# Broadcasting the reciprocal RMS of a window: from two TensorE transposes and a ScalarE copy to a round trip through DRAM

## The chip, the cores and the metric

The kernel runs on one core of a Trainium2 chip. The metric is the device time of one execution in microseconds (us). TensorE is written PE here, VectorE DVE, ScalarE ACT, GpSimd POOL and SyncE SP, as the profile writes them.

## The reference

One inference step of a two-layer decoder trunk, for a prompt of 4096 tokens and a sample group of 8 sequences with 4 tokens each; the model width is 1024. Both layers begin with an RMS norm over the 1024 features of each token, and it is the factor of this norm that the change sends another way:

```
def rms_norm(x, g):
    xf = x.astype(jnp.float32)
    y = xf * lax.rsqrt(jnp.mean(xf * xf, axis=-1, keepdims=True) + NORM_EPS)
    return (y * g.astype(jnp.float32)).astype(x.dtype)
```

Layer 0 projects the normed input to an S5 branch (a diagonal complex recurrence over the tokens, followed by GELU and a gated unit) and to a GLA branch (gated linear attention in chunks of 64 tokens), joins the two, projects them back and adds the residual. Layer 1 projects to 16 query heads and 2 key and value heads, applies norms and a rotary embedding, attends within a window of 128 tokens with a sink per head, multiplies with a gate, projects back and adds the residual. Weights and activations are float32 at the border; the kernel splits each operand of a projection into a high and a low float16 part and multiplies three of the four products.

## The kernel before, in words

The activations lie with the features on the partitions and the tokens along the free axis. A window is 256 tokens (`NW`), of which the prompt has 16; the 1024 features of one window are four chunks of 128 partitions by 2 by 256 float32, 256 KB each.

The program has three phases. **Phase 0** (up to about 420 us, with loads to about 600) computes the weights' scales, the S5 tables, the S5 projection of all windows (`stage`, then `ustream`) and the S5 scan. `stage` also computes the reciprocal RMS of each window of the input and keeps it in `rst0`, with the tokens on the partitions: column 2w holds the first 128 tokens of window w, column 2w+1 the others. **Phase 1** (about 600 to 1750 us) goes through the windows of layer 0; the end of a window (`outstream`) writes the layer's result to DRAM (`h1_d`), sums its squares, and `stats` and `rms` keep the reciprocal RMS for layer 1 in `rst1`. **Phase 2** (about 1800 us to the end) goes through the windows of layer 1, with input chunks loaded from `h1_d`.

A window begins with `prep`. Four input chunks, which were loaded when the window before began, have to be multiplied by the reciprocal RMS of their tokens. Since tokens lie along the free axis there, the 256 factors are needed as a row on all 128 partitions. `rbcast` (L294 to L304) makes that tile, `rb`: two PE transposes (L300) of a `rst` column, broadcast along its free axis, into a PSUM tile, and one ACT copy (L303) to SBUF. `xsplit` (L306 to L318) then handles each chunk in three steps: DVE multiplies it by `rb` (L313), ACT rounds it to the high part `xh` (L314), POOL subtracts to get the low part `xl` (L315). All projections of the window read `xh` and `xl` on PE.

The reciprocal RMS itself comes out of `rms` (L285 to L292): a sum of squares on PE, a scale and an offset on DVE (`var`, L291), and a power of -1/2 on POOL (`rst`, L292).

Each engine executes its own instructions in order. The order is set when the program is built: `merge` interleaves generators that stand for streams of work by the costs that they yield, and a scheduler then places each instruction on its engine by modelled times. Tiles come from pools with a number of buffers each; an instruction that writes a tile waits until the last reader of the buffer's former content is done. SP issues nearly all the DMAs, and it does so in order as well: a DMA whose source or buffer isn't ready holds up every DMA behind it.

Of the kernel before, what the change touches and what calls it, by code (L numbers as in the profile page):

```python
# [106 lines left out]
class K:  # L107
# [166 lines left out]

    def stats(self, acc, n, rst, blk0, wp, pp, tag="misc"):

        nc = self.nc
        nc.gpsimd.tensor_add(acc[:, 0, 0:n], acc[:, 0, 0:n], acc[:, 1, 0:n])
        m = min(n, 128)
        ps = pp.tile([128, 512], F32, name=tag)  # L280
        for i in range((n + 127) // 128):
            nc.tensor.matmul(ps[0:m, i:i + 1], acc[:, 0, i * 128:i * 128 + m], self.onesf[:, 0:1], start=True, stop=True)
        self.rms(ps, n, rst, blk0, wp)

    def rms(self, ps, n, rst, blk0, wp):  # L285

# [316 lines left out]
    def phase0(self):  # L603
# [50 lines left out]
        for k in range(KT):  # L654
            nc.scalar.activation(wuh[:, k], st[k], AF.Copy, bias=0.0, scale=gs[:, k:k + 1])
            nc.vector.scalar_tensor_tensor(wul[:, k], st[k], gs[:, k:k + 1], wuh[:, k],
                                           op0=OP.mult, op1=OP.subtract)

        def stage(c0, n, blk0, xs=None):

# [3 lines left out]
            for c in range(4):  # L664
# [169 lines left out]
    def phase1(self, es0, tail):  # L834
# [90 lines left out]
        def prep(w):  # L925
            rb = self.rbcast(self.rst0, 2 * w, n, Pb, pmi, tag="pt")
            Ws[w]["x"] = self.xsplit(Ws[w]["x"], n, rb, hp)
            if w + 1 < NWIN:
                Ws[w + 1]["x"] = self.xload(xp, I["xT"], n * (w + 1), n)

        def gate_a(w):
# [424 lines left out]
        def outstream(W, w):  # L1356
# [91 lines left out]
    def phase2(self, es1, tail):  # L1448
# [703 lines left out]
```

## Time and profile before

| what | value |
|---|---|
| median of 3 runs | 3215.05 us (3214.31 to 3219.88) |
| the profiled execution's own time | 3223.62 us |
| its span, first to last instruction | 3221.8 us |
| mean granted TensorE clock | 0.975 |
| PE busy | 3048.6 us, 95% of the span |
| DVE busy | 2016.0 us, 63% |
| ACT busy | 1504.0 us, 47% |
| POOL busy | 1304.7 us, 40% |
| hardware DMA queue, share of 16 engines | 36.5% |

The times of the three runs and that of the profiled execution belong to the same kernel; the profiled one is 8.57 us above the median. Busy shares are means over the whole span, in which phase 0 differs from the other two phases: there PE, DVE and POOL take turns as the busiest engine, while PE is the busiest by far in phases 1 and 2.

### The profile page before, as it was taken

How to read it: one execution, taken by the hardware profiler on the slowest of the kernel's cores; microseconds unless marked ns; L12 is line 12 of the kernel's file. 1: busy time of each engine (PE TensorE's matmuls, PEld its weight loads, DVE VectorE, ACT ScalarE, POOL GpSimd, SP SyncE). 2: the span in 40 equal slices, each digit the busy share in tenths (PEclk: the TensorE clock that was granted, in tenths of full speed). 3: DMA queues.
4: the chain of work that ended last, by engine and by line, in shares of the span. 5: the costliest groups of instructions: out<-in, count | busy, mean ns of one | idle time of the engine just before them, and what ended most of it. 6: DMA issues, size and time to landing. Idle time of an engine off the chain costs nothing. (4 is left out here: it accounts for less than half of the span.)

```text
span 3221.8 us, 65657 instructions
## 1 busy us (share of the span) xinstructions
PE 3048.6 (95%) x25501; PEld 2351.8 (73%) x25501; DVE 2016.0 (63%) x4881; ACT 1504.0 (47%) x3954; POOL 1304.7 (40%) x1324
## 2 busy tenths in 40 slices
PE   6898878899999999999999999999999999999998
PEld 5687766678888777788877666777677777777777
DVE  8869998744444443444446567666666666666666
ACT  4386557343343443333345345444445454444444
POOL 7823232222222211222222555555555555555562
PEclk9699989999999999999999989999999999999999
DMA  4288467622222222322224325333333333333333
GB/s 131 56 233 195 97 143 195 185 54 56 53 54 57 55 52 65 71 57 53 50 49 138 100 48 129 80 79 80 75 75 77 79 74 80 74 81 79 82 77 77
DMA packets 583467, 285.57 MB, mean 89 GB/s; under 512 B 396497, under 2 KB 556193, under 8 KB 583009
## 3 DMA queue, kind: packets, MB, share of 16 engines
q1 hardware_dynamic: 583152, 281.36, 36.5%
q8 instruction: 200, 3.28, 0.4%
q14 instruction: 115, 0.93, 0.1%
HBM read 164.94 MB, written 53.23 MB: 68 GB/s over the span
## 5 line engine op out<-in xcount | busy, mean ns | idle before, releaser
L315 POOL TENSOR_TENSOR xl<-x,xh 128x512 f16<-128x512 f32 (+1 forms) x196 | 261.3, 1356 | 301.3 <-ACT xh L314 273.5
L1687 ACT ACTIVATE Sc<-Sc,ng,rq 128x128 f32<-128x128 f32 x512 | 245.8, 482 | 163.7 <-DVE ng L1681 159.6
L326 PE MATMUL mm<-ogh,woh 128*128 128x256 f16 x960 | 261.5, 273 | 3.5 <-ACT vf L1627 3.0
L327 PE MATMUL mm<-ogl,woh 128*128 128x256 f16 x960 | 261.6, 273 | 0.0
L328 PE MATMUL mm<-ogh,wol 128*128 128x256 f16 x960 | 261.6, 273 | 0.0
L273 POOL TENSOR_TENSOR acc<-acc,sq 128x512 f32<-128x512 f32 x48 | 62.4, 1300 | 489.7 <-ACT sq L272 489.7
L1716 POOL TENSOR_TENSOR Pp<-Sc,Pp 128x512 f16<-128x512 f32 x128 | 151.9, 1188 | 210.3 <-ACT Pp L1715 200.9
L326 PEld LDWEIGHTS <-woh 128*128 128x128 f16 x2112 | 207.4, 98 | 39.8 <-issue 10.4
L327 PEld LDWEIGHTS <-woh 128*128 128x128 f16 x2112 | 207.4, 98 | 38.6 <-issue 9.8
L337 PEld LDWEIGHTS <-xl 128*128 128x128 f16 x1536 | 150.9, 98 | 111.7 <-issue 15.3
L328 PEld LDWEIGHTS <-wol 128*128 128x128 f16 x2112 | 207.2, 98 | 28.0 <-issue 4.8
L335 PEld LDWEIGHTS <-xh 128*128 128x128 f16 x1536 | 151.2, 98 | 99.3 <-issue 13.4
L336 PEld LDWEIGHTS <-xh 128*128 128x128 f16 x1536 | 151.1, 98 | 89.4 <-issue 5.9
L1723 DVE TENSOR_TENSOR PC<-PT,mT 128x1024 f16<-128x1024 f16 x128 | 100.4, 784 | 162.6 <-DMA PT<-Pp 158.3
L314 ACT ACTIVATE xh<-x 128x512 f16<-128x512 f32 (+1 forms) x196 | 118.1, 618 | 118.9 <-DVE x L313 102.9
L326 PE MATMUL mm<-xh,wuh 128*128 128x256 f16 (+1 forms) x544 | 151.1, 282 | 10.3 <-ACT us L728 4.9
L327 PE MATMUL mm<-xl,wuh 128*128 128x256 f16 (+1 forms) x544 | 150.5, 282 | 6.9 <-POOL xl L315 6.9
L313 DVE TENSOR_TENSOR x<-x,rb 128x512 f32<-128x512 f32 (+1 forms) x188 | 138.4, 789 | 20.9 <-ACT rb L303 12.9
L328 PE MATMUL mm<-xh,wul 128*128 128x256 f16 (+1 forms) x544 | 150.5, 282 | 0.0
L1715 ACT ACTIVATE Pp<-Sc 128x512 f16<-128x512 f32 x128 | 80.1, 626 | 141.0 <-issue 115.9
L328 PE MATMUL mm<-xh,wi1gal 128*128 128x256 f16 x512 | 141.1, 276 | 4.0 <-DVE wi1gal L246 4.0
L326 PE MATMUL mm<-xh,wi1qkh 128*128 128x256 f16 x512 | 140.2, 274 | 4.8 <-DVE gb L963 4.8
(724 smaller groups left out, 10487.8 us busy)
## 6 DMA issues: line engine op xcount, KB each, us to landing
x<-in_xT SPq DMA_DIRECT2D x128, 256.0 KB
wst<-in_w_in SPq DMA_DIRECT2D x64, 256.0 KB
xr<-in_xT SPq DMA_DIRECT2D x64, 256.0 KB
h_d<-xr SPq DMA_DIRECT2D x64, 256.0 KB
x<-h_d SPq DMA_DIRECT2D x64, 256.0 KB
xr<-h_d SPq DMA_DIRECT2D x64, 256.0 KB
out_yT<-xr SPq DMA_DIRECT2D x64, 256.0 KB
wst<-in_w_out SPq DMA_DIRECT2D x48, 256.0 KB
```

Of the source, the lines that this page charges most:

```text
L313: nc.vector.tensor_mul(x, x, rb[:, None, :].to_broadcast([128, 2, n]))
L314: nc.scalar.activation(h, x, AF.Copy, bias=0.0, scale=1.0)
L315: nc.gpsimd.tensor_sub(l, x, h)
L326: nc.tensor.matmul(ps, wh[:, k0 + k, c], xh[k], start=(k == 0), stop=False)
L327: nc.tensor.matmul(ps, wh[:, k0 + k, c], xl[k], start=False, stop=False)
L328: nc.tensor.matmul(ps, wl[:, k0 + k, c], xh[k], start=False, stop=(k == n - 1))
L335: nc.tensor.matmul(ps, xh[k][:, t], wh[:, k, c0:c1], start=(k == 0), stop=False)
L336: nc.tensor.matmul(ps, xh[k][:, t], wl[:, k, c0:c1], start=False, stop=False)
L337: nc.tensor.matmul(ps, xl[k][:, t], wh[:, k, c0:c1], start=False, stop=(k == n - 1))
L1687: nc.scalar.activation(Sc[:, i], Sc[:, i], AF.Exp, bias=ng[:, i:i + 1], scale=scale[:, i:i + 1], accum_out=de[:, i:i + 1])
L1716: nc.gpsimd.tensor_sub(Pp[:, 1], Sc, Pp[:, 0])
L1723: nc.vector.tensor_mul(PC, PT, mT[:, None, :].to_broadcast([128, 8, 128]))
```

## The change

`rms` gets a destination. When it has computed the factors of a window other than window 0, POOL issues a DMA that writes the window's two columns to a DRAM row of 256 float32 (`rs0` for layer 0, `rs1` for layer 1). That is 15 writes in phase 0 and 15 in phase 1, of 256 elements of 4 bytes each (the column pair is read with the partition as the inner axis). A new function `rbload` reads such a row to all 128 partitions by a DMA on SP, whose source has a step of 0 along the partitions: 1 KB of DRAM becomes a tile of 128 KB. `prep` of phases 1 and 2 takes this tile in place of the result of `rbcast`. In phase 1 it is loaded a window ahead, right behind the four input chunks; in phase 2 the program loads it in `prep` itself. `rb` has one buffer.

`rbcast` is still used for window 0 of phases 1 and 2, for the `split` of phase 0 (all 16 windows of the S5 projection) and for both sample groups.

```
--- before.py
+++ after.py
@@ -272,7 +272,7 @@
             nc.scalar.activation(sq, x, AF.Square, bias=0.0, scale=1.0)
             nc.gpsimd.tensor_add(acc[:, :, 0:n], acc[:, :, 0:n], sq)
 
-    def stats(self, acc, n, rst, blk0, wp, pp, tag="misc"):
+    def stats(self, acc, n, rst, blk0, wp, pp, tag="misc", dst=None):
 
         nc = self.nc
         nc.gpsimd.tensor_add(acc[:, 0, 0:n], acc[:, 0, 0:n], acc[:, 1, 0:n])
@@ -280,9 +280,9 @@
         ps = pp.tile([128, 512], F32, name=tag)
         for i in range((n + 127) // 128):
             nc.tensor.matmul(ps[0:m, i:i + 1], acc[:, 0, i * 128:i * 128 + m], self.onesf[:, 0:1], start=True, stop=True)
-        self.rms(ps, n, rst, blk0, wp)
-
-    def rms(self, ps, n, rst, blk0, wp):
+        self.rms(ps, n, rst, blk0, wp, dst)
+
+    def rms(self, ps, n, rst, blk0, wp, dst=None):
 
         nc = self.nc
         nb = (n + 127) // 128
@@ -290,6 +290,14 @@
         v = wp.tile([128, 2], F32, name="var")
         nc.vector.tensor_scalar(v[0:m, 0:nb], ps[0:m, 0:nb], 2.0**-20 / D, 2.0**-20 * EPS, op0=OP.mult, op1=OP.add)
         nc.gpsimd.tensor_tensor(rst[0:m, blk0:blk0 + nb], v[0:m, 0:nb], self.mhalf[0:m, 0:nb], op=OP.pow)
+        if dst is not None and nb == 2 and blk0:
+            nc.gpsimd.dma_start(dst[blk0 // 2].rearrange("b p -> p b"), rst[:, blk0:blk0 + 2])
+
+    def rbload(self, d, pool, bufs=1):
+
+        rb = pool.tile([128, NW], F32, name="rb", bufs=bufs)
+        self.nc.sync.dma_start(rb, bass.AP(tensor=d.tensor, offset=d.offset, ap=[[0, 128], [1, NW]]))
+        return rb
 
     def rbcast(self, rst, blk0, n, wp, pp, tag="misc", rtag="rb", **kw):
 
@@ -656,6 +664,9 @@
             nc.vector.scalar_tensor_tensor(wul[:, k], st[k], gs[:, k:k + 1], wuh[:, k],
                                            op0=OP.mult, op1=OP.subtract)
 
+        self.rs0 = [self.dr.tile([2, 128], F32, name=f"rs0_{w}") for w in range(NWIN)]
+        self.rs1 = [self.dr.tile([2, 128], F32, name=f"rs1_{w}") for w in range(NWIN)]
+
         def stage(c0, n, blk0, xs=None):
 
             xs = xs or self.xload(xp, I["xT"], c0, n)
@@ -682,7 +693,7 @@
                     for i in range((n + 127) // 128):
                         nc.tensor.matmul(ps[0:m, i:i + 1], sq[:, a, 128 * i:128 * i + m], self.onesf[:, 0:1],
                                          start=(c + a + i == 1), stop=(c + a == 4), skip_group_check=True)
-            self.rms(ps, n, self.rst0, blk0, wp)
+            self.rms(ps, n, self.rst0, blk0, wp, self.rs0)
 
             def split():
                 rb = self.rbcast(self.rst0, blk0, n, wp, pms)
@@ -923,10 +934,11 @@
         n = NW
 
         def prep(w):
-            rb = self.rbcast(self.rst0, 2 * w, n, Pb, pmi, tag="pt")
+            rb = Ws[w]["rb"]
             Ws[w]["x"] = self.xsplit(Ws[w]["x"], n, rb, hp)
             if w + 1 < NWIN:
                 Ws[w + 1]["x"] = self.xload(xp, I["xT"], n * (w + 1), n)
+                Ws[w + 1]["rb"] = self.rbload(self.rs0[w + 1], Pb)
 
         def gate_a(w):
             W = Ws[w]
@@ -1367,7 +1379,7 @@
                 if c == 0:
                     W["r"].append(self.xchunk(P, I["xT"], 3, n * w, n, name="xr", bufs=3))
             yield 0.1
-            self.stats(acc, n, self.rst1, 2 * w, P, pms, tag="pt")
+            self.stats(acc, n, self.rst1, 2 * w, P, pms, tag="pt", dst=self.rs1)
 
         def glu(w, early):
             W = Ws[w]
@@ -1409,6 +1421,7 @@
         Ws = [{} for _ in range(NWIN)]
         Ws[0]["x"] = x0
         Ws[1]["x"] = self.xload(xp, I["xT"], n, n)
+        Ws[1]["rb"] = self.rbload(self.rs0[1], Pb)
         merge((instream(0), 42.0), (loads(), 20.0))
 
         def some(g, n):
@@ -1528,7 +1541,7 @@
         self.vf = None
 
         def prep(w):
-            rb = self.rbcast(self.rst1, 2 * w, n, Pa, ptt, tag="pt")
+            rb = self.rbload(self.rs1[w], Pa)
             Ws[w]["x"] = self.xsplit(Ws[w]["x"], n, rb, hp)
             if w + 1 < NWIN:
                 Ws[w + 1]["x"] = self.xload(xp, self.h1_d, n * (w + 1), n)

```

(The prompt's window 0 keeps the old way since `x0` of phase 0 is passed on, and the first window of phase 2 is handled apart.)

Counted over the built programs, the change takes away 60 PE transposes (24183 matmuls become 24123) and 30 ACT copies, and adds 30 DMAs on SP (1197 become 1227) and 30 DMAs on POOL, which issued none before. Lines behind the new code move: L313 is L321 in the changed kernel, L315 is L323, L1354 is L1366.

The scheduler places the remaining instructions anew. Three places follow; numbers behind a name tell buffers and values apart.

The first is DVE at the end of a window of phase 1, where the residual chunks `xr` of this window are summed and the input chunks `x` of the next are multiplied by `rb`. Before:

```order
L1354 SCALAR_TENSOR_TENSOR xr_11522<-mm_12177,sob_5387,xr_11522 128x512
L1354 SCALAR_TENSOR_TENSOR xr_11524<-mm_12243,soa_5411,xr_11524 128x512
L1354 SCALAR_TENSOR_TENSOR xr_11524<-mm_12281,sob_5387,xr_11524 128x512
L1354 SCALAR_TENSOR_TENSOR xr_12080<-mm_12341,soa_5411,xr_12080 128x512
L313 TENSOR_TENSOR x_11472<-x_11472,rb_12372 128x512
L313 TENSOR_TENSOR x_11474<-x_11474,rb_12372 128x512
L313 TENSOR_TENSOR x_11476<-x_11476,rb_12372 128x512
L313 TENSOR_TENSOR x_11478<-x_11478,rb_12372 128x512
L1354 SCALAR_TENSOR_TENSOR xr_12080<-mm_12405,sob_5387,xr_12080 128x512
L1103 COPY_PREDICATED attm0_5376<-mk_5372,pa0_12687 128x256
```

In the changed kernel:

```order
L1366 SCALAR_TENSOR_TENSOR xr_10630<-mm_11356,soa_5458,xr_10630 128x512
L1366 SCALAR_TENSOR_TENSOR xr_10630<-mm_11394,sob_5434,xr_10630 128x512
L321 TENSOR_TENSOR x_11504<-x_11504,rb_11510 128x512
L321 TENSOR_TENSOR x_11506<-x_11506,rb_11510 128x512
L1366 SCALAR_TENSOR_TENSOR xr_11193<-mm_11454,soa_5458,xr_11193 128x512
L321 TENSOR_TENSOR x_11508<-x_11508,rb_11510 128x512
L1366 SCALAR_TENSOR_TENSOR xr_11193<-mm_11515,sob_5434,xr_11193 128x512
L321 TENSOR_TENSOR x_12422<-x_12422,rb_12430 128x512
L1068 SCALAR_TENSOR_TENSOR A_11604<-A_11604,z_11559 128x256
```

The block of four multiplications is taken apart: they stand between the `xr` rows, each behind its own chunk's load, and the first chunk of the window after next (`x_12422`, with the next `rb`, `rb_12430`) follows at once. On SP, `rb_12430` stands behind the load of `x_12422`, and behind it the store of `xr_11193` to `h1_d`, a load of `xr` and four loads of `z`; as `rb` has one buffer, that DMA waits for the multiplication of `x_11508`.

The second is DVE in a window of phase 2, where the softmax of a block (`mx`, `ng`, `sn`, `de`, `Sc`) stands among the multiplications. Before:

```order
L313 TENSOR_TENSOR x_24068<-x_24068,rb_25249 128x512
L313 TENSOR_TENSOR x_24070<-x_24070,rb_25249 128x512
L313 TENSOR_TENSOR x_24072<-x_24072,rb_25249 128x512
L1712 COPY_PREDICATED Sc_25279<-mkc_20886,pt_25280 128x256
L1767 SCALAR_TENSOR_TENSOR og_25093<-po_25080,ga_23923 128x256
L1767 SCALAR_TENSOR_TENSOR og_25093<-po_25080,ga_23984 128x256
L1712 COPY_PREDICATED Sc_25279<-mkc_20886,pt_25291 128x256
L1712 COPY_PREDICATED Sc_25473<-mkc_20886,pt_25474 128x256
L1677 TENSOR_REDUCE mx_25302<-Sc_25279 128x4
L1712 COPY_PREDICATED Sc_25473<-mkc_20886,pt_25485 128x256
L1678 TENSOR_TENSOR mx_25302<-mx_25302,rq_24146 128x4
L313 TENSOR_TENSOR x_24074<-x_24074,rb_25249 128x512
```

In the changed kernel:

```order
L1690 TENSOR_REDUCE mx_27707<-Sc_27684 128x4
L321 TENSOR_TENSOR x_26482<-x_26482,rb_27654 128x512
L1691 TENSOR_TENSOR mx_27707<-mx_27707,rq_26554 128x4
L1692 TENSOR_TENSOR mx_27707<-mx_27707,snk_20901 128x4
L1780 SCALAR_TENSOR_TENSOR og_27501<-po_27488,ga_26334 128x256
L1780 SCALAR_TENSOR_TENSOR og_27501<-po_27488,ga_26395 128x256
L1694 TENSOR_SCALAR ng_27711<-mx_27707 128x4
L1696 TENSOR_TENSOR sn_27713<-ng_27711,snk_20901 128x4
L321 TENSOR_TENSOR x_27676<-x_27676,rb_28923 128x512
L321 TENSOR_TENSOR x_27678<-x_27678,rb_28923 128x512
L1703 TENSOR_TENSOR de_27768<-de_27768,sn_27713 128x4
```

The window's last chunk (`x_26482`, with `rb_27654`) and the first chunks of the next window (`x_27676`, with `rb_28923`) now stand six rows apart, all of one softmax chain. The load of `rb_28923` waits on SP for the multiplication of `x_26482`, the last that reads the one buffer.

The third is POOL in phase 0, where the S5 tables are made (`tv`, `tc`, `tg`) and the low parts of the S5 projection's input. Before:

```order
L315 TENSOR_TENSOR xl_1437<-x_1293,xh_1436 128x512
L292 TENSOR_TENSOR rst0_76<-var_1525,mhalf_74 128x2
L499 TENSOR_TENSOR tv_1148<-Q2_493,R81_665 128x512
L528 TENSOR_TENSOR tc2_529<-CT1_93,sn_445 128x8x32
L492 TENSOR_TENSOR tg_994<-bc_293,Li_119 128x576
L526 TENSOR_TENSOR tc1_528<-ST1_94,sn_445 128x8x32
L499 TENSOR_TENSOR tv_1197<-Q2_493,R81_665 128x512
L492 TENSOR_TENSOR tg_1019<-bc_293,Li_119 128x576
```

In the changed kernel:

```order
L292 TENSOR_TENSOR rst0_76<-var_1560,mhalf_74 128x2
L507 TENSOR_TENSOR tv_1182<-Q2_526,R81_698 128x512
L536 TENSOR_TENSOR tc2_562<-CT1_93,sn_478 128x8x32
L500 TENSOR_TENSOR tg_1028<-bc_325,Li_119 128x576
L534 TENSOR_TENSOR tc1_561<-ST1_94,sn_478 128x8x32
L507 TENSOR_TENSOR tv_1231<-Q2_526,R81_698 128x512
L294 DMA rs0_4_246<-rst0_76 128x2x1
L500 TENSOR_TENSOR tg_1053<-bc_325,Li_119 128x576
L534 TENSOR_TENSOR tc1_561<-ST1_94,sn_478 128x512
```

The write of `rs0_4` stands between two table instructions, six rows behind the power that makes its source; the table instructions themselves stand in nearly the same order.

## Rows read from the trace of the kernel before

**Rows 1.** Busy time of each engine by stretch; its first line names the columns.
```profile
core 0: us, PE busy (x) PEld busy (x) DVE busy (x) ACT busy (x) POOL busy (x), PEclk, DMA share, GB/s
40.00:160.00 120.00, 95.53 (x630) 77.58 (x628) 108.10 (x178) 41.12 (x73) 107.20 (x70) 0.75 0.28 62
160.00:220.00 60.00, 55.36 (x463) 49.58 (x461) 27.77 (x43) 45.16 (x97) 18.82 (x16) 0.91 0.83 220
220.00:420.00 200.00, 169.38 (x1409) 151.23 (x1406) 198.27 (x380) 124.71 (x261) 64.58 (x46) 0.96 0.66 156
600.00:1700.00 1100.00, 1088.82 (x9185) 858.63 (x9182) 483.46 (x1257) 436.26 (x1034) 249.12 (x217) 1.00 0.24 60
1850.00:3222.00 1372.00, 1329.70 (x11411) 976.86 (x11409) 909.48 (x2312) 656.41 (x2064) 732.35 (x836) 0.99 0.37 79
```

**Rows 2.** PE's waits from 600 to 1700 us: waiting line, releaser, us in total, times, longest.
```profile
PE mm L326 <- DVE xr L1354: 4.2, 2, 2.1
PE pt L282 <- POOL acc L278: 3.0, 1, 3.0
...
PE mm L327 <- POOL xl L315: 0.8, 2, 0.5
```

**Rows 3.** PE's waits from 1850 us to the end, the same columns.
```profile
PE po L1761 <- DMA PT<-Pp: 26.8, 22, 3.2
PE mm L326 <- ACT vf L1627: 3.0, 1, 3.0
...
PE mm L337 <- POOL xl L315: 0.8, 1, 0.8
```

**Rows 4.** Timeline of PE, phase 1: start us, us, instruction, count, idle before.
```profile
1004.48 0.27 PE L327 MATMUL mm<-ol,woh 128*128 128x256 f16 x1
1004.59 0.27 PE L328 MATMUL mm<-oh,wol 128*128 128x256 f16 x1
1004.70 0.38 PE L300 MATMUL pt<-identf,rst 128*128 128x128 f32 x2
1004.92 0.27 PE L326 MATMUL mm<-ob,woh 128*128 128x256 f16 x1
1005.03 0.27 PE L327 MATMUL mm<-ob,woh 128*128 128x256 f16 x1
```

**Rows 5.** Timeline of ACT, phase 1.
```profile
1005.12 0.38 ACT L303 ACTIVATE rb<-pt 128x256 f32<-128x256 f32 x1 [2.15 <-PE pt L300]
```

**Rows 6.** Timeline of DVE, phase 1, end of a window.
```profile
997.10 0.75 DVE L1354 SCALAR_TENSOR_TENSOR xr<-mm,sob,xr 128x512 f32<-128x512 f32 x1 [4.24 <-PE mm L328]
1004.90 0.75 DVE L1354 SCALAR_TENSOR_TENSOR xr<-mm,soa,xr 128x512 f32<-128x512 f32 x1 [7.05 <-PE mm L328]
1005.57 3.45 DVE L313 TENSOR_TENSOR x<-x,rb 128x512 f32<-128x512 f32 x4
1008.94 0.74 DVE L1354 SCALAR_TENSOR_TENSOR xr<-mm,sob,xr 128x512 f32<-128x512 f32 x1
```

**Rows 7.** Timeline of SP in phase 2.
```profile
2647.51 6.15 SPq L259 DMA_DIRECT2D x<-h_d  x4
2658.18 1.23 SPq L1718 DMA_TRANSPOSE PT<-Pp  x1
2659.99 0.38 SPq L1807 DMA_DIRECT2D out_yT<-xr  x1
```

**Rows 8.** Timeline of DVE, phase 2, around a chunk's multiplication.
```profile
2646.71 0.75 DVE L1767 SCALAR_TENSOR_TENSOR og<-po,ga 128x256 f32<-128x256 f32 x2
...
2649.02 0.71 DVE L1678 TENSOR_TENSOR mx<-mx,rq 128x4 f32<-128x4 f32 x1
2650.38 0.99 DVE L313 TENSOR_TENSOR x<-x,rb 128x512 f32<-128x512 f32 x1 [0.65 <-DMA x<-h_d]
...
2651.90 0.15 DVE L1679 TENSOR_TENSOR mx<-mx,snk 128x4 f32<-128x4 f32 x1
...
2652.09 0.16 DVE L1681 TENSOR_SCALAR ng<-mx 128x4 f32<-128x4 f32 x1
...
2653.21 0.15 DVE L1683 TENSOR_TENSOR sn<-ng,snk 128x4 f32<-128x4 f32 x1
```

**Rows 9.** Timeline of POOL, phase 0.
```profile
124.48 5.54 POOL L528 TENSOR_TENSOR tc<-CT,sn 128x512 f32<-128x512 f32 x1
...
137.97 0.69 POOL L292 TENSOR_TENSOR rst<-var,mhalf 128x2 f32<-128x2 f32 x1
...
143.38 1.49 POOL L528 TENSOR_TENSOR tc<-CT,sn 128x512 f32<-128x512 f32 x1
```

**Rows 10.** Timeline of SP, phase 0.
```profile
173.03 1.29 SPq L737 DMA_DIRECT2D ud<-us  x2
...
179.51 0.97 SPq L760 DMA_DIRECT2D U<-ud  x2
```

**Rows 11.** Timeline of DVE, phase 0: the last table instruction.
```profile
157.76 0.69 DVE L530 TENSOR_TENSOR ST<-ST,tc 128x512 f32<-128x512 f32 x1
```

**Rows 12.** Page, part 5: the group of the softmax products on DVE.
```profile
L1723 DVE TENSOR_TENSOR PC<-PT,mT 128x1024 f16<-128x1024 f16 x128 | 100.4, 784 | 162.6 <-DMA PT<-Pp 158.3
```

More of the change, by code (lines that the diff above doesn't have):

```diff
@@ L273, in square, with stats @@
             nc.gpsimd.tensor_add(acc[:, :, 0:n], acc[:, :, 0:n], sq)
-    def stats(self, acc, n, rst, blk0, wp, pp, tag="misc"):
+    def stats(self, acc, n, rst, blk0, wp, pp, tag="misc", dst=None):
         nc = self.nc
@@ L282, in stats, with rms @@
             nc.tensor.matmul(ps[0:m, i:i + 1], acc[:, 0, i * 128:i * 128 + m], self.onesf[:, 0:1], start=True, stop=True)
-        self.rms(ps, n, rst, blk0, wp)
-    def rms(self, ps, n, rst, blk0, wp):
+        self.rms(ps, n, rst, blk0, wp, dst)
+    def rms(self, ps, n, rst, blk0, wp, dst=None):
         nc = self.nc
@@ L292, in rms, with rbload @@
         nc.gpsimd.tensor_tensor(rst[0:m, blk0:blk0 + nb], v[0:m, 0:nb], self.mhalf[0:m, 0:nb], op=OP.pow)
+        if dst is not None and nb == 2 and blk0:
+            nc.gpsimd.dma_start(dst[blk0 // 2].rearrange("b p -> p b"), rst[:, blk0:blk0 + 2])
+    def rbload(self, d, pool, bufs=1):
+        rb = pool.tile([128, NW], F32, name="rb", bufs=bufs)
+        self.nc.sync.dma_start(rb, bass.AP(tensor=d.tensor, offset=d.offset, ap=[[0, 128], [1, NW]]))
+        return rb
     def rbcast(self, rst, blk0, n, wp, pp, tag="misc", rtag="rb", **kw):
@@ L657, in phase0 @@
                                            op0=OP.mult, op1=OP.subtract)
+        self.rs0 = [self.dr.tile([2, 128], F32, name=f"rs0_{w}") for w in range(NWIN)]
+        self.rs1 = [self.dr.tile([2, 128], F32, name=f"rs1_{w}") for w in range(NWIN)]
         def stage(c0, n, blk0, xs=None):
@@ L684, in stage @@
                                          start=(c + a + i == 1), stop=(c + a == 4), skip_group_check=True)
-            self.rms(ps, n, self.rst0, blk0, wp)
+            self.rms(ps, n, self.rst0, blk0, wp, self.rs0)
             def split():
@@ L925, in prep @@
         def prep(w):
-            rb = self.rbcast(self.rst0, 2 * w, n, Pb, pmi, tag="pt")
+            rb = Ws[w]["rb"]
             Ws[w]["x"] = self.xsplit(Ws[w]["x"], n, rb, hp)
@@ L929, in prep @@
                 Ws[w + 1]["x"] = self.xload(xp, I["xT"], n * (w + 1), n)
+                Ws[w + 1]["rb"] = self.rbload(self.rs0[w + 1], Pb)
         def gate_a(w):
@@ L1369, in outstream @@
             yield 0.1
-            self.stats(acc, n, self.rst1, 2 * w, P, pms, tag="pt")
+            self.stats(acc, n, self.rst1, 2 * w, P, pms, tag="pt", dst=self.rs1)
         def glu(w, early):
@@ L1411, in phase1 @@
         Ws[1]["x"] = self.xload(xp, I["xT"], n, n)
+        Ws[1]["rb"] = self.rbload(self.rs0[1], Pb)
         merge((instream(0), 42.0), (loads(), 20.0))
@@ L1530, in prep @@
         def prep(w):
-            rb = self.rbcast(self.rst1, 2 * w, n, Pa, ptt, tag="pt")
+            rb = self.rbload(self.rs1[w], Pa)
             Ws[w]["x"] = self.xsplit(Ws[w]["x"], n, rb, hp)
```

## The prediction

> **What bounds the kernel now.** I read the busy time by stretch first [rows 1]. From 600 to 1700 us PE is busy for 1088.82 of 1100 us, from 1850 us to the end for 1329.70 of 1372; the granted clock is 1.00 and 0.99 there, the upper of its two levels. DVE has 483.46 and 909.48 us of work in the same stretches, ACT 436.26 and 656.41, POOL 249.12 and 732.35. So PE sets the time in both phases, and an edit counts there by what it does to PE's stream or to PE's waits. Then I read those waits. In phase 1 they are few, the largest 4.2 us for sums of the residual (`xr`) in two waits [rows 2]; none is for `rb`. In phase 2 one stands out: PE's product `po` waits for the transposed softmax `PT` for 26.8 us, in 22 waits of at most 3.2 us [rows 3]. The group of DVE's products on the same `PT` has 128 members [rows 12], so about one block in six is late. The chain that makes these blocks runs over DVE, ACT, POOL and SP, so what delays DVE in phase 2 can show on PE.
>
> Phase 0 is different. Between 40 and 160 us POOL is busy for 107.20 of 120 us and DVE for 108.10, PE for 95.53 [rows 1]; from 220 to 420 us DVE is busy for 198.27 of 200. Between the two, the 60 us up to 220 have DVE at 27.77 and POOL at 18.82, while the DMAs take a share of 0.83. The tables end on DVE at 158.4 us [rows 11], but S5's first loads of `U` are issued only at 179.5, behind a store of `ud` at 173.0 [rows 10]. The tables are thus ready some 20 us before they are wanted, and the low parts (`xl`) of the S5 projection and the DMAs decide.
>
> **What goes.** On PE, a pair of transposes starts at 1004.70 and the next matmul at 1004.92: 0.22 us of its stream, in which two matmuls of the usual kind would fit [rows 4]. No wait of PE is put down to them in phases 1 and 2. With 60 transposes gone, 30 pairs x 0.22 = 6.6 us leave the bounding engine, 3.3 us per phase. On ACT 30 copies go, 0.38 us each [rows 5], together 11.4 us; ACT has 1100 - 436.26 us free in phase 1 alone, so this is worth nothing by itself. It did wait 2.15 us in order for the transpose, and this wait goes too; but the four multiplications that follow on DVE take 3.45 us [rows 6], and PE waited only 0.8 us for any `xl` in each of the two phases [rows 2, 3]. A shorter way to `xl` therefore gives at most 1.6 us; I take 0.
>
> **What comes: the writes, on POOL.** Thirty DMAs are issued by POOL, which issued none before, so the trace has no price. From below: SP's plain DMA takes 0.38 us to issue [rows 7], if POOL does as well. From above: POOL's instructions sometimes take several times their length, as the 5.54 us for a `tc` that takes 1.49 a few rows on [rows 9]; if a write is stretched by that difference as well, it is 0.38 + 4.05 = 4.4 us. I take the transposing DMA on SP, 1.23 us [rows 7], as the nearest row, since it also scatters single elements. In the stretch in which POOL is nearly full stand four writes (`rs0_2` to `rs0_5`): 1.5, 4.9 or 17.7 us. The 20 us between tables and `U` hide the middle value, as far as it delays tables; the low parts in the same stretch have no such slack that a row shows, so I take 0 and keep 0 to 17.7 us for the range. The other 11 writes of phase 0 and the 15 of phase 1 stand where POOL has most of its time free (249.12 of 1100 us busy), and their results are wanted a phase later. They cost nothing there. Each moves 1 KB.
>
> The Trainium skill speaks against exactly this issue: "SBUF — State Buffer", in "SBUF: two separate sides", says that a DMA issued from POOL has its descriptors made by POOL's cores, which can't write them while DVE runs an instruction that takes both ports; its figures are some 620 ns alone and some 3100 ns beside a DVE copy. The stretched POOL rows in a time of a busy DVE agree in kind [rows 9], though no run here shows a DMA of POOL. By its two figures, called an estimate here, four writes would take 2.5 to 12.4 us, inside the bounds above.
>
> **What comes: the loads, on SP and DVE.** Thirty loads x 0.38 us are 11.4 us of SP's issue time in some 2500 us, and 128 KB each are 3.8 MB where the DMA share is 0.24 and 0.37 [rows 1]. Nothing for these. What counts is the wait: `rb` has one buffer, so its load starts when the last multiplication with the former tile is done, and DVE then stands in order until it has landed. For the time of a load the nearest row is that of the input chunk, 256 KB: the first of a group of four is issued at 2647.51, and the multiplication that waited for one began at 2650.38 [rows 7, 8], so issue and load took at most 2.87 us. I take 2.9 us from the former multiplication's end to the next one's start; the lower bound is half of it, as the transfer has half the bytes.
>
> In phase 1, between the two multiplications (`x_11508` and `x_12422`) stands one sum of `xr`, which waits for PE. In the trace of before such a sum waited 4.24 and 7.05 us for PE [rows 6], more than 2.9. The load lies in the shadow of a wait that is there anyway: 0. Behind it on SP, the store of `xr`, one load of `xr` and four of `z` come later by up to 2.9 us; the `xr` load is the one that PE could come to feel, through a sum of the next window; PE's 4.2 us in two waits for such sums [rows 2] show how seldom they are late, and I take 0.
>
> In phase 2, six rows stand between: two of `mx`, two of `og`, one `ng`, one `sn`. By their rows that is 0.71 + 0.15 + 0.75 (for both `og`) + 0.16 + 0.15 = 1.92 us [rows 8]. DVE would stand 2.9 - 1.9 = 1.0 us in the middle of a softmax chain, with `de` and `Sc` queued behind, on which POOL, the transposing DMA and at last PE's `po` wait. From below it is 0 (the load at half the time). Before, DVE stood 0.65 us there for an input chunk [rows 8], so not all of this is new. With 15 windows that is 15 us for DVE, of which PE feels what falls on a block that is late already: 22 of 128 [rows 3, 12], so 15 x 0.17 = 2.6 us. That is the term I take; the bounds are 0 and 15 us.
>
> **The reordering.** The scheduler shifts matmuls by a few places in all phases. No row prices this. PE's waits of 12 us in phase 1 and some 40 in phase 2 (1100 - 1088.82 and 1372 - 1329.70) are the size of what it can give or take; I take 0 and allow 6 us either way.
>
> **The sum.** -6.6 + 0 + 2.6 = -4.0 us. The profiled execution would go from 3223.62 to 3219.6 us (its span of 3221.8 has 1.8 us around it, which do not change). The median of the runs is 8.57 us below that execution, and I lower it by the same 4.0: 3215.05 - 4.0 = 3211.0 us. That is 0.12%. A measurement of this kernel tells about 0.2% from no change, which is 6.4 us: faster means below 3208.6, slower above 3221.5.
>
> **The rivals.**
> *A larger gain.* The transposes' and the copy's waits in order are gone, multiplications start as soon as a chunk lands, and the softmax chain of the next window finds ACT and DVE free. If a third of PE's 26.8 us for `PT` goes too, it is -6.6 - 8.9 = -15.5: 3199.5 us. For it: DVE's block of 3.45 us is taken apart, and it held up the next sum [rows 6]. Against it: PT's wait has no `rb` in it.
> *The wait for rb decides phase 2.* DVE stands for 1.0 us in each of 15 windows, and each of these delays goes through the softmax chain to PE, in place of one in six: 15 - 6.6 = +8.4: 3223.5 us. It decides from the point where more than 6.6 us of the 15 reach PE, and shows as slower from 13. For it: one buffer, and the chain is the one wait that PE has [rows 3]. Against it: only 22 of 128 blocks are late now.
> *The writes lengthen phase 0.* Four stretched writes at 4.4 us, all on the path through the low parts to `U`: 17.7 - 4.0 = +13.7: 3228.8 us. It shows as slower from 10.4 us on, 2.6 us a write. For it: POOL's 107.20 of 120 us [rows 1]. Against it: the 20 us between the tables and `U` [rows 10, 11].
> *The change doesn't do what it says.* What PE saves it waits for elsewhere, as the chain over DVE, POOL and SP keeps its length: 3215 us. Phase 1 speaks against it, where PE is at 99% [rows 1].
>
> **How the numbers follow.** The forecast has 0.45, the larger gain 0.20, the wait in phase 2 0.15, the writes 0.12, nothing 0.08. Of the forecast's 0.45, with its 6 us either way, 0.18 falls below 3208.6 and 0.26 within the 0.2%, 0.01 above. Faster: 0.18 + 0.20 = 0.38. Same: 0.26 + 0.08 = 0.34. Slower: 0.15 + 0.12 + 0.01 = 0.28. The range runs from 3196 (a little beyond the larger gain) to 3230 us (a little beyond the writes). The forecast's own range is 3205 to 3217.
>
> **What would show it.** Right: PE's busy time in phases 1 and 2 lower by some 6 us; no PE wait on `rb` or its multiplication; the multiplications of phase 1 late by nothing on the `rb` DMA; `PT` waits near 27 to 30 us. Wrong: a wait of DVE for the `rb` load above 1 us per window and PE's `PT` waits above 35 us (the second rival); POOL's spans between 40 and 160 us longer and the first `U` load later than 179.5 us (the third); `PT` waits below 20 us (the first); equal PE busy time but longer PE waits in both phases (the last).

## The result, and the profile after

The changed kernel takes 3327.94 us in the median (3315.84 to 3331.53, 4 runs) against 3215.32 us (3214.31 to 3219.88; 4 runs, one more than in the table ahead) for the kernel before: a ratio of 1.0335, with a 95% interval of 1.0314 to 1.0356. It is 113 us slower, where the prediction had 4 us faster and a range that ended at 3230. The profiled execution took 3330.15 us, with a span of 3328.4.

The busy times of the changed kernel by stretch, the counterpart of [rows 1]; the stretches are moved with the phases, and the first line names the columns:

```profile
core 0: us, PE busy (x) PEld busy (x) DVE busy (x) ACT busy (x) POOL busy (x), PEclk, DMA share, GB/s
40.00:160.00 120.00, 99.28 (x647) 79.23 (x646) 105.40 (x176) 42.75 (x75) 110.71 (x75) 0.73 0.41 62
160.00:420.00 260.00, 189.18 (x1482) 167.87 (x1482) 176.66 (x336) 145.79 (x310) 71.57 (x62) 0.85 0.75 150
660.00:1850.00 1190.00, 1156.11 (x9647) 911.21 (x9646) 484.16 (x1329) 463.98 (x1097) 254.24 (x240) 0.98 0.25 62
2000.00:3328.00 1328.00, 1279.31 (x10965) 938.52 (x10961) 885.57 (x2213) 627.64 (x1978) 689.87 (x797) 0.99 0.37 81
```

Until 160 us little has changed: POOL has 110.71 us of work where it had 107.20 [rows 1]. From 160 to 420 us DVE is busy for 176.66 of 260 us; before, it was busy for 226.04 of the same 260 us (27.77 + 198.27 [rows 1]). In phase 1 PE is busy for 97.2% of the stretch, where it had been 99.0%. In phase 2 its share is 96.3%, and was 96.9%. PE's own work takes longer too: by the pages it is busy for 3072.3 us with 60 transposes fewer, and was for 3048.6. The granted clock is 0.85 from 160 to 420 us, where it was 0.91 up to 220 and 0.96 after [rows 1], and PE stands idle for 27% of that stretch.

How much each phase lost is seen from three groups of instructions that end a phase. The last store of `ud`, which ends the S5 projection, starts at 411.7 us before and at 467.7 now: 56 us are lost in phase 0. The last `var` of phase 1 stands at 1806.1 and at 1902.7: another 41 us. The last `PC` stands at 3204.0 and 3310.4: another 10. Each pair shows first the kernel before, then the changed one (duration in ns: least, median, most; first and last start in us):

```profile
L737 SPq DMA_DIRECT2D ud<-us x32: 513/610/1085, 58.9 to 411.7; - x32
L748 SPq DMA_DIRECT2D ud<-us x32: 513/647/1586, 60.7 to 467.7; - x32
...
L291 DVE TENSOR_SCALAR var<-pt x17: 141/151/158, 624.4 to 1806.1; 128x2 f32<-128x2 f32 x16, 32x1 f32<-32x1 f32 x1
L291 DVE TENSOR_SCALAR var<-pt x17: 147/159/160, 680.6 to 1902.7; 128x2 f32<-128x2 f32 x16, 32x1 f32<-32x1 f32 x1
...
L1723 DVE TENSOR_TENSOR PC<-PT,mT x128: 674/692/1573, 1836.8 to 3204.0; 128x1024 f16<-128x1024 f16 x128
L1736 DVE TENSOR_TENSOR PC<-PT,mT x128: 677/693/1681, 1935.9 to 3310.4; 128x1024 f16<-128x1024 f16 x128
```

PE's waits from 600 to 1900 us, the counterpart of [rows 2] (waiting line, releaser, us in total, times, longest), and from 1950 us to the end, that of [rows 3]:

```profile
PE pt L1141 <- DVE S L1143: 28.6, 11, 5.9
PE pt L978 <- ACT al L972: 3.6, 1, 3.6
PE mm L334 <- DVE xr L1366: 3.3, 2, 2.8
```

```profile
PE po L1774 <- DMA PT<-Pp: 37.5, 24, 2.9
PE mm L343 <- DVE ga L1569: 1.8, 1, 1.8
```

The first row is new (before, such a wait came to 0.2 us): PE waits 28.6 us, nearly 6 at the longest, for `S`, the state of GLA, which DVE updates. `PT` went from 26.8 to 37.5 us. DVE's waits for the loaded `rb` are there as well, in phase 1 and in phase 2:

```profile
DVE x L321 <- DMA rb<-rs: 24.1, 11, 2.7
```

```profile
DVE x L321 <- DMA rb<-rs: 5.3, 6, 2.4
```

And this is the group of the 30 writes on POOL (duration in ns: least, median, most; first and last start):

```profile
L294 POOL DMA_DIRECT2D rs<-rst x30: 737/757/937, 41.4 to 1903.9; - x30
...
DMA to landing us min/median/max: 8.3/9.6/12.1
```

To issue one costs POOL 0.76 us, between the bounds of the prediction. But it takes 8.3 to 12.1 us until 1 KB has landed.

### The profile page after: what moved, and what is told of

It reads as the page before. It is cut to its first block, busy times and chain, and to the rows that moved or that the text cites. A ratio compares the mean times of both kernels' runs of the same rounds, so it can differ in the third digit from the quotient of the medians.

```text
span 3328.4 us, 65624 instructions
## 1 busy us (share of the span) xinstructions
PE 3072.3 (92%) x25441; PEld 2363.7 (71%) x25441; DVE 1988.2 (60%) x4881; ACT 1493.0 (45%) x3922; POOL 1297.3 (39%) x1354
## 5 line engine op out<-in xcount | busy, mean ns | idle before, releaser
L323 POOL TENSOR_TENSOR xl<-x,xh 128x512 f16<-128x512 f32 (+1 forms) x196 | 242.8, 1260 | 249.2 <-ACT xh L322 241.8
L1736 DVE TENSOR_TENSOR PC<-PT,mT 128x1024 f16<-128x1024 f16 x128 | 107.2, 837 | 178.6 <-DMA PT<-Pp 176.5
L321 DVE TENSOR_TENSOR x<-x,rb 128x512 f32<-128x512 f32 (+1 forms) x188 | 132.0, 730 | 124.4 <-POOL xl L323 40.5
L344 PE MATMUL mm<-wi1gbl,xh 128*128 128x264 f16 x512 | 146.4, 286 | 4.3 <-DVE wi1gbl L246 4.3
L343 PE MATMUL mm<-wi1gbh,xh 128*128 128x264 f16 x512 | 146.0, 286 | 1.0 <-DVE ga L954 0.7
```

What stands on the lines that cost most here:

```text
L321: nc.vector.tensor_mul(x, x, rb[:, None, :].to_broadcast([128, 2, n]))
L323: nc.gpsimd.tensor_sub(l, x, h)
L343: nc.tensor.matmul(ps, xh[k][:, t], wh[:, k, c0:c1], start=(k == 0), stop=False)
L344: nc.tensor.matmul(ps, xh[k][:, t], wl[:, k, c0:c1], start=False, stop=False)
L1736: nc.vector.tensor_mul(PC, PT, mT[:, None, :].to_broadcast([128, 8, 128]))
```

## The experiments

Three theories stood against each other. A: the scheduler's new order of phase 0 is worse, and DVE's wait for `rb` costs in phase 1. B: writes through POOL's software queue slow the core's other DMAs. C: the loads and their waits cost, not the writes. A fourth, D, came out of the first runs below. Each kernel is compared with runs of the kernel before on the same chip; ratios have 95% intervals. The diffs are excerpts: each shows the lines that make the difference.

**One half of the change, or one part of it.** `layer1_only` leaves phases 0 and 1 as they were but for the writes of `rst1`:

```diff
-            self.rms(ps, n, self.rst0, blk0, wp, self.rs0)
+            self.rms(ps, n, self.rst0, blk0, wp)
...
-            rb = Ws[w]["rb"]
+            rb = self.rbcast(self.rst0, 2 * w, n, Pb, pmi, tag="pt")
```

> Only layer 1's half of the change: 15 writes of rst1 on POOL in phase 1, 15 loads in phase 2; phases 0 and 1 keep the transposes. Phase 0 stands in exactly the order of the kernel before on DVE, ACT and SP. Theory A (the new order of phase 0 costs some 55 us, the in-order wait for rb in phase 1 some 43, phase 2 some 10): phase 0 ends as before, phase 1 as before, total 3215 + 0 to 10 = 3215 to 3225 us. Theory B (a software-queue write slows the core's other DMAs from then on): phase 1 and 2 are longer, 3240 us or more. Theory C (what costs is the loads and DVE's wait in either phase): about half of the phase-1 loss in phase 2, 3225 to 3240 us.

Measured: 3271.45 us, ratio 1.0174 (1.0154 to 1.0194). Half of the loss is there, with phase 0 in its old order. A and C named at most 3240, B more.

`writes_only` keeps all the writes and takes the loads away:

```diff
-            rb = self.rbload(self.rs1[w], Pa)
+            rb = self.rbcast(self.rst1, 2 * w, n, Pa, ptt, tag="pt")
```

(and the same in phase 1).

> All 30 writes on POOL stay, nothing loads them, and prep uses the transposes again in both phases. Phase 0's order is nearly that of the changed kernel (97% of DVE's rows, 92% of SP's). Theory A: phase 0 is late as in the changed kernel (the last store of ud near 465 us in place of 412), phase 1 and 2 as before: 3265 to 3275 us. Theory B: the same in phase 0 and also longer phases 1 and 2. Theory C (loads): 3215 to 3222 us, phase 0 as before.

Measured: 3327.62 us, ratio 1.0341 (1.0319 to 1.0363), as slow as the whole change. With that the loads are not what makes the loss: C has fallen.

`loads_only` takes the writes away and loads a constant row of the input, so it leaves out the norm of windows 1 to 15:

```diff
-        self.rs0 = [self.dr.tile([2, 128], F32, name=f"rs0_{w}") for w in range(NWIN)]
+        self.rs0 = [I["xT"][0:1, 0:256]]
```

> No writes; all 30 loads read one constant row of the input in place of the factors, so the norm of windows 1 to 15 is left out of the computation. Phase 0's order is near that of the kernel before (96% of DVE's rows, 88% of SP's). Theory A: phase 0 ends within 10 us of before, phase 1 longer by some 43 us, phase 2 by 10: 3260 to 3275 us. Theory B: all is as before, 3208 to 3220 us. Theory C: 3260 to 3275, from DVE's wait for the rb load in phase 1.

Measured: 3225.48 us, ratio 1.0034 (1.0021 to 1.0047). Some 10 us slower than before, all parts of the saving included: A had put 43 us on DVE's wait for `rb` and the new order of phase 1. In the profiled executions, one of each kernel, the loss isn't in phase 1, which takes 1387.9 us from the last `ud` store to the last `var` (1394.4 before), but in phase 2, with 1408.4 from there to the last `PC` (1397.9 before).

`dummy128` is to show what a new order alone does:

```diff
-            nc.gpsimd.dma_start(dst[blk0 // 2].rearrange("b p -> p b"), rst[:, blk0:blk0 + 2])
+            dm = wp.tile([128, 128], F32, name="dm", bufs=2)
+            nc.gpsimd.tensor_copy(dm, rst[:, blk0:blk0 + 1].to_broadcast([128, 128]))
```

> No write and no load. After each power of phase 0 (15 times) POOL copies a factor to a scratch tile of 128 by 128 that nothing reads; the transposes stay. The scheduler places phase 0 anew (80% of DVE's rows and 66% of SP's as before). Theory A (the order decides, not the DMA): the time moves by tens of us either way although the work is only 15 x about 0.3 us on POOL; a time within 6 us of 3215 speaks against it. Theory B and C: 3215 to 3222 us.

Measured: 3224.99 us, ratio 1.0023 (1.0010 to 1.0037). This order, which isn't that of the changed kernel, moves the time by some 9 us (3 to 12 by the interval), more than B and C said and less than A. What the changed kernel's own order can cost at most is seen further down (`writes_row8`, `row8`).

**The write by itself.** The order of the kernel before can be kept if only phase 1's writes are added, since POOL has room there. The kernels named `w1_` do so, with 99.7% to 100% of the rows in the old order. `w1_pool` adds the 15 writes of `rst1` as the change has them, and nothing reads them:

```diff
+            nc.gpsimd.dma_start(dst[blk0 // 2].rearrange("b p -> p b"), rst[:, blk0:blk0 + 2])
```

> The kernel before with 15 writes added and nothing else: in phase 1 POOL writes the two columns of rst1 to DRAM, as in the changed kernel, and nothing reads them. The order on every engine is that of the kernel before (99.7% to 100% of the rows). Theory B (each software-queue write slows the hardware DMAs beside it, the four z loads above all, by some 3.5 us that reach PE): 15 x 3.5 = 53 us more, 3265 to 3272 us, with z loads that take 6 us to issue in place of 3. Theory A (the order decides): 3215 to 3218 us.

Measured: 3269.16 us, ratio 1.0161 (1.0139 to 1.0182): 3.5 us for each write of 1 KB. What happens is seen around the first of them. POOL, SP, ACT, DVE and PE in the trace of `w1_pool`, with the start, the duration, and in brackets the idle time before and what ended it:

```profile
704.21 0.94 POOL L294 DMA_DIRECT2D rs<-rst  x1 [0.31 <-POOL rst L292]
...
710.26 6.41 SPq L1388 DMA_DIRECT2D z<-zd  x4
...
717.02 0.72 ACT L1050 ACTIVATE zo<-z,wz_p 128x256 f16<-128x256 f32 x1 [4.70 <-DMA z<-zd]
...
717.77 0.65 DVE L1051 SCALAR_TENSOR_TENSOR zo<-z,wz_p,zo 128x256 f16<-128x256 f32 x1 [4.74 <-ACT zo L1050]
718.34 0.33 DVE L1142 SCALAR_TENSOR_TENSOR S<-S,sc,pt 128x128 f32<-128x128 f32 x1
...
718.73 0.44 PE L1140 MATMUL pt<-v,kT 128*64 128x128 f32 x4 [2.84 <-DVE S L1142]
```

The same loads and what follows them in the trace of the kernel before:

```profile
713.19 3.07 SPq L1377 DMA_DIRECT2D z<-zd  x4
...
715.99 0.74 ACT L1039 ACTIVATE zo<-z,wz_p 128x256 f16<-128x256 f32 x1 [0.74 <-DMA z<-zd]
...
716.76 0.66 DVE L1040 SCALAR_TENSOR_TENSOR zo<-z,wz_p,zo 128x256 f16<-128x256 f32 x1 [0.79 <-ACT zo L1039]
717.34 0.34 DVE L1131 SCALAR_TENSOR_TENSOR S<-S,sc,pt 128x128 f32<-128x128 f32 x1
```

The four loads of `z` take 6.41 us to issue and not 3.07. From their issue to the first `zo` on ACT it is 6.76 us (717.02 - 710.26) where it was 2.80 (715.99 - 713.19). DVE stands in order before its own `zo` for 4.74 us, with the update of `S` queued behind, and PE waits 2.84 us for that `S`. The stretches of `w1_pool` from 704 us on (columns: the stretch, PE, PEld, DVE, ACT, POOL, clock, DMA share, GB/s) say where the loads were:

```profile
704.00:706.00 2.00, 2.00 (x21) 1.79 (x20) 0.94 (x2) 1.21 (x3) 1.77 (x2) 1.00 0.05 9
706.00:708.00 2.00, 2.00 (x21) 1.80 (x19) 0.82 (x1) 0.00 (x0) 0.35 (x1) 1.00 0.00 0
708.00:710.00 2.00, 2.00 (x21) 1.79 (x19) 0.38 (x1) 0.56 (x1) 0.00 (x0) 1.00 0.00 0
710.00:712.00 2.00, 2.00 (x20) 1.79 (x19) 0.98 (x2) 0.89 (x2) 0.18 (x1) 1.00 0.00 1
712.00:714.00 2.00, 2.00 (x22) 1.57 (x23) 0.69 (x1) 0.32 (x1) 0.97 (x1) 1.00 0.00 0
714.00:716.00 2.00, 1.89 (x17) 1.40 (x15) 0.00 (x0) 0.00 (x0) 0.00 (x0) 1.00 0.29 47
716.00:718.00 2.00, 0.00 (x0) 0.00 (x0) 0.23 (x1) 0.98 (x4) 0.00 (x0) 1.00 1.10 166
```

The DMA engines moved next to nothing until 714 us, although the `z` loads were being issued from 710.26 on. The write, issued at 704.21, takes 10.0 us to land in the median here: the loads start about when it is done. By the profile the engines aren't busy with the write in that time: their share is 0.05 from 704 to 706 us and 0.00 from there to 714. So a busy share doesn't show this wait, and where on its way the write spends it no run shows.

Other windows of the same trace tell how the distance counts. A write 2.67 us ahead of the `z` loads, and one 12.16 us ahead:

```profile
948.90 0.76 POOL L294 DMA_DIRECT2D rs<-rst  x1 [0.30 <-POOL rst L292]
...
951.57 8.19 SPq L1388 DMA_DIRECT2D z<-zd  x4
...
1296.94 0.76 POOL L294 DMA_DIRECT2D rs<-rst  x1 [0.29 <-POOL rst L292]
...
1309.10 2.84 SPq L1388 DMA_DIRECT2D z<-zd  x4
```

The nearer the write, the longer the issue of the loads: 8.19 us at 2.67, 6.41 at 6.05, and 2.84, as before, at 12.16.

`w1_sp` sends the same write from SP, by the hardware queue:

```diff
-            nc.gpsimd.dma_start(dst[blk0 // 2].rearrange("b p -> p b"), rst[:, blk0:blk0 + 2])
+            nc.sync.dma_start(dst[blk0 // 2].rearrange("b p -> p b"), rst[:, blk0:blk0 + 2])
```

> The same 15 writes, of the same 256 elements of 4 bytes each, issued by SP through the hardware queue in place of POOL; the order elsewhere is that of the kernel before. If the software queue is what costs: 3213 to 3222 us (SP waits in order for the power, which delays the z loads by a little). If the 256 scattered elements of 4 bytes cost, on whichever queue: 3250 us or more.

Measured: 3267.22 us, ratio 1.0157 (1.0135 to 1.0178), and the same picture. SP in `w1_sp`:

```profile
704.62 0.37 SPq L294 DMA_DIRECT2D rs<-rst  x1
710.94 5.72 SPq L1388 DMA_DIRECT2D z<-zd  x4
```

Its DMAs, too, move nothing until 714 us:

```profile
712.00:714.00 2.00, 2.00 (x22) 1.54 (x22) 0.69 (x1) 1.00 (x2) 1.16 (x1) 1.00 0.00 1
```

So it isn't the software queue, and B fell as it was put. What both kernels have in common are 256 elements of 4 bytes. `w1_row8` keeps the layout of the source, so that each partition sends one run of 8 bytes, and `w1_one` sends a single run of 1 KB:

```diff
-            nc.gpsimd.dma_start(dst[blk0 // 2].rearrange("b p -> p b"), rst[:, blk0:blk0 + 2])
+            d = dst[blk0 // 2]
+            nc.gpsimd.dma_start(bass.AP(tensor=d.tensor, offset=d.offset, ap=[[2, 128], [1, 2]]), rst[:, blk0:blk0 + 2])
```

> The same 15 writes on POOL, but in the layout of the source, so that each partition sends one run of 8 bytes: 128 runs in place of 256. If the cost goes with the number of elements that POOL describes: half, about 3240 us. If any software-queue write costs the same: 3265 to 3272 us.

> POOL's 15 writes send one contiguous run of 1 KB from a single partition (a row of acc, whose values nothing reads) in place of 256 elements. If the cost goes with the number of elements: 3215 to 3220 us. If any software-queue write costs the same, whatever it moves: 3265 to 3272 us.

Measured: 3221.18 us, ratio 1.0011 (0.9999 to 1.0022), and 3217.52 us, ratio 0.9999 (0.9986 to 1.0012). Both are about as fast as the kernel before; of half the cost, which was to show if the number of elements decides, nothing is seen. The write of `w1_one` doesn't wait for the power that makes `rst` and stands some 9 us ahead of the `z` loads in most windows, so its time says less than its landing does. `w1_col` has the number of runs of `w1_row8` and the run size of `w1_pool`, one column of 128 elements of 4 bytes:

```diff
+            nc.gpsimd.dma_start(bass.AP(tensor=d.tensor, offset=d.offset, ap=[[1, 128], [1, 1]]), rst[:, blk0:blk0 + 1])
```

> Fifteen writes in phase 1 of one column only: 128 elements of 4 bytes to 512 contiguous bytes, half of the factors, which nothing reads. It tells the number of runs from their size: if the number decides, the write lands in some 3.6 us as with 128 runs of 8 bytes and the time is 3215 to 3222 us; if runs of 4 bytes are slow in themselves, it lands in some 6 us and the time is 3225 to 3250 us.

Measured: 3263.74 us, ratio 1.0147 (1.0123 to 1.0171), above both of the ranges expected. Here is the time to landing in `w1_pool`, `w1_col`, `w1_row8` and `w1_one` (least, median and most, in us):

```profile
DMA to landing us min/median/max: 8.3/10.0/10.7
```

```profile
DMA to landing us min/median/max: 6.9/7.7/10.0
```

```profile
DMA to landing us min/median/max: 3.1/3.6/4.5
```

```profile
DMA to landing us min/median/max: 1.6/2.5/3.3
```

The size of the run decides more than their number: 128 runs of 4 bytes take 7.7 us, 128 of 8 bytes 3.6. Half of the bytes cost almost all of the time, 3.1 us a write where 256 runs cost 3.5. The `z` loads come some 6 us behind the write, before it has landed; but 7.7 us to landing would leave 1.7 us of waiting, so the landing time alone doesn't give the 3.1. What these kernels leave is theory D: a write in runs of 4 bytes holds up, for some 8 to 10 us, the DMAs issued behind it.

`w1_quiet` puts the write of 256 elements of 4 bytes where no urgent DMA follows, behind the first square of a window:

```diff
                 self.square(x, c, acc, P, n)
+                if c == 0 and w:
+                    nc.gpsimd.dma_start(self.rs1[w].rearrange("b p -> p b"), acc[:, 0, 0:2])
```

> The kernel before with 15 writes of 256 elements of 4 bytes on POOL, as in w1_pool, but of the first two columns of acc after its first square, some 40 us ahead of the z loads; nothing reads them. The order of all other instructions is that of the kernel before. Theory D with the z loads as the victims: 3213 to 3222 us, and z loads that take about 3 us to issue. If the write costs wherever it stands: 3260 us or more.

Measured: 3220.42 us, ratio 1.0010 (1.0000 to 1.0019), with a landing time of 9.5 us in the median as before. SP's row for the `z` loads in `w1_quiet`, 48 us behind the write at 739.77:

```profile
787.76 2.81 SPq L1388 DMA_DIRECT2D z<-zd  x4
```

The same write, as long as ever, now costs at most some 6 us in all: what is paid for in phase 1 is the `z` loads behind it.

**Phase 0, and the whole change with other runs.** `writes_row8` is `writes_only` with runs of 8 bytes, in the same order on every engine; the edit is that of `w1_row8`.

> The kernel writes_only again, in exactly its order on every engine, but each of the 30 writes on POOL sends 128 runs of 8 bytes in place of 256 of 4. Theory D (a write of 256 scattered elements of 4 bytes holds up all DMAs behind it for some 8 us, 15 times in phase 0 and 15 times in phase 1): most of the 112 us is gone, 3215 to 3235 us, with the first loads of U and the end of phase 0 near those of the kernel before. Theory A for phase 0 (there the new order costs): 3265 to 3275 us.

Measured: 3237.08 us, ratio 1.0058 (1.0039 to 1.0076), 2 us above the range of theory D. 90 of the 112 us are gone, in the same order; the last store of `ud` starts at 422.9 us, and in `writes_only` at 463.7:

```profile
L748 SPq DMA_DIRECT2D ud<-us x32: 513/610/1236, 60.8 to 463.7; - x32
...
L749 SPq DMA_DIRECT2D ud<-us x32: 512/660/1247, 58.7 to 422.9; - x32
```

So phase 0 too pays for the 4-byte runs. It shows in the loads of `U`. SP and POOL in the changed kernel:

```profile
185.26 0.74 POOL L294 DMA_DIRECT2D rs<-rst  x1 [0.29 <-POOL rst L292]
...
189.66 7.66 SPq L771 DMA_DIRECT2D U<-ud  x3
...
204.22 0.74 POOL L294 DMA_DIRECT2D rs<-rst  x1 [0.29 <-POOL rst L292]
...
208.37 9.28 SPq L771 DMA_DIRECT2D U<-ud  x5
```

The same two groups of loads in `writes_row8`:

```profile
188.08 1.99 SPq L772 DMA_DIRECT2D U<-ud  x3
...
203.99 3.45 SPq L772 DMA_DIRECT2D U<-ud  x5
```

Behind a write in 4-byte runs SP spends 7.66 us on three loads of `U` and 9.28 on five; with 8-byte runs it is 1.99 and 3.45.

`writes_tiny` sends four runs of 8 bytes, in nearly the same order:

```diff
-ap=[[2, 128], [1, 2]]), rst[:, blk0:blk0 + 2])
+ap=[[2, 4], [1, 2]]), rst[0:4, blk0:blk0 + 2])
```

> All 30 writes on POOL, of four runs of 8 bytes each (the factors of 8 tokens; nothing reads them), no loads; 96% to 99.9% of the rows stand in the order of writes_row8. If the 20 us that are left there are the order's: 3228 to 3240 us. If they are the writes' (128 runs landing in 3.5 us): 3214 to 3222 us.

Measured: 3226.93 us, ratio 1.0031 (1.0018 to 1.0044), between the two answers. Of the 20 us, some 11 stay with nearly nothing written, as in `dummy128`, and go to the order and POOL's issue; the rest may be the 128 runs, but the intervals of the two kernels overlap.

`row8` is the whole change with runs of 8 bytes. The row in DRAM then has the two halves of the window interleaved, and DVE reads the tile with a step of two:

```diff
+        return rb.rearrange("q (p b) -> q b p", b=2)
...
+                xv = x.rearrange("q k (b p) -> q k b p", b=2)
+                nc.vector.tensor_mul(xv, xv, rb[:, None, :, :].to_broadcast([128, 2, 2, 128]))
```

> The whole change, with one difference: the writes keep the layout of the source (runs of 8 bytes), and DVE reads the broadcast tile with a step of two elements. The order is that of the changed kernel on every engine. Theory D: 3218 to 3235 us, as the loads alone took 3225. Theory A: 3265 us or more. If the strided read slows DVE's 120 multiplications, they take over 0.75 us where they took 0.69.

Measured: 3231.94 us, ratio 1.0048 (1.0032 to 1.0064); a multiplication takes 693 ns in the median, and 684 with the unstrided tile. PE is busy for 3044.0 us there, 28 less than in the changed kernel with as many instructions, and the granted clock from 160 to 420 us is 0.92: the slower clock goes with the 4-byte runs. `row8_l1` does this for layer 1 alone and leaves phase 0's order:

> Only layer 1's half of the change, with writes in runs of 8 bytes; phase 0 stands in the order of the kernel before. Theory D: the 56 us of the same half with runs of 4 bytes are gone, and what is left is the saving of 15 x 0.22 = 3.3 us and DVE's wait for the load: 3208 to 3220 us. If it is below 3212 it beats the kernel before.

Measured: 3218.47 us, ratio 1.0002 (0.9989 to 1.0015). No version beat the kernel before.

## Why the prediction was wrong

The step that failed is the one on the writes. It priced them by POOL's time to issue, and set the rest aside: "their results are wanted a phase later. They cost nothing there. Each moves 1 KB." The issue was priced well, at 0.76 us between 0.38 and 4.4. Missing was the time for which such a write holds up the DMAs issued behind it, some 8 to 10 us. The share of the DMA engines, 0.24 in phase 1 [rows 1], could not tell of it: it is a mean, and it is 0.00 while `w1_pool`'s loads wait. In phase 1 the writes cost 3.5 us each, 53 us for 15 (`w1_pool`), in place of 0. In phase 0 they cost some 40 us (`writes_only` less `writes_row8` is 90 us for both phases, less 3269.16 - 3221.18 = 48 for phase 1; the last store of `ud` gives 463.7 - 422.9 = 41), in place of 0 with a bound of 17.7. The write's place was looked at only on POOL; which loads are issued within the next 10 us, those of `U` and `z`, was not asked.

The rule cited from the Trainium skill ("SBUF — State Buffer", in "SBUF: two separate sides", on descriptors that POOL's cores can't write) did not decide. `w1_sp` issues the write from SP and is as slow, and POOL's issue never took over 0.94 us. The Trainium skill's page "DMA: Bandwidth & Descriptors", in "Rules for kernel authors", has a rule that bears on this write: a last dimension that isn't contiguous becomes one descriptor per element. The runs agree in kind, 10.0 us to landing for 256 single elements and 3.6 for 128 pairs (`w1_pool`, `w1_row8`); but 128 single elements take 7.7 (`w1_col`), so the number of pieces alone doesn't give the times.

The other steps:
- *The saving of 6.6 us.* Neither confirmed nor refuted: no kernel shows it apart. With 8-byte runs the kernel with loads took 3231.94 us and the one with transposes 3237.08, a difference of the right sign whose intervals overlap; `row8_l1`, where 3.3 us should go, is within its interval of no change. PE's busy time doesn't show it either: 3044.0 us in `row8`, 3042.8 in `writes_row8`.
- *DVE's wait for `rb` in phase 1, forecast at 0.* Wrong for DVE, which waits 24.1 us in 11 waits, though a sum of `xr` stands between. As a cost in time the 0 isn't refuted: `loads_only` has 16.8 us of this wait, and its phase 1 is no longer than that of before (1387.9 and 1394.4 us).
- *The wait in phase 2, forecast at 15 us on DVE and 2.6 on PE.* DVE waits 5.3 us there, in 6 waits. `PT`'s waits went from 26.8 [rows 3] to 37.5 us, past the 35 us that were to be the mark of the second rival, and are 41.0 in `loads_only`. But `row8_l1` has the same loads in phase 2 and 28.1 us of these waits; which part is the loads is open.
- *The reordering, allowed 6 us either way.* Too little for phase 0: `dummy128` and `writes_tiny` are 9 and 11 us slower with next to no work added.
- *The rival on the writes* had the right object and the wrong resource. Its mark, a first load of `U` later than 179.5 us, did show (189.66), but it tells little of the writes: that load stands at 188.08 us in `writes_row8` and at 186.14 in `dummy128`, which writes nothing. And its price of 17.7 us was counted in POOL's time.

In sum, 96 of the 113 us are the 4-byte runs' (3327.94 - 3231.94, the changed kernel less `row8`, in the same order but on another chip). `row8` itself is 15 us slower than its own runs of the kernel before: that is what the change costs with 8-byte runs. A new order of phase 0 cost 9 to 11 us in `dummy128` and `writes_tiny`; that it is most of these 15 is likely, not shown. Why a run of 4 bytes is so much slower than one of 8 stays open.

## What to carry to other kernels

Price a DMA by what stands behind it, not by its bytes or its issue: read when it lands, and which loads on the critical path are issued until then. Keep an SBUF-to-DRAM store in the layout of the source, so that a partition sends one run of 8 bytes or more, and put the reordering on the reader's access pattern; here that took 96 of 113 us away. Where a scattered store can't be avoided, place it where no urgent load follows for some 12 us, the longest time to landing seen here.

## What the runs showed of the hardware

A store of 1 KB as 256 runs of 4 bytes took 8 to 12 us to land, and loads issued 6 us behind it moved next to nothing until 714 us, 9 to 10 us after its issue, whether POOL or SP had issued the store (`w1_pool`, `w1_sp`). The share of the DMA engines in that time was 0.00, so a small share is no sign that a load will start at once. At 128 runs, 4 bytes took 7.7 us and 8 bytes 3.6; a single run of 1 KB took 2.5. SP's own issue of the next DMAs was held up as well, 6.41 us for four in place of 3.07.
